# A gated DeltaNet layer on one core: another split of the PSUM banks and longer delays in a hand-set TensorE order

## The chip, the core and the metric

The kernel runs on one core of a Trainium2 chip. The core has five engines with instruction streams of their own: PE (TensorE, matrix products into PSUM), DVE (VectorE), ACT (ScalarE), POOL (GpSimd) and SP (SyncE, which here issues every DMA). The metric is the device time of one execution in microseconds (us), and the median over runs is compared.

## What is computed

One layer of a decoder trunk with 1024 tokens of 1024 features, 16 value heads and 8 query/key heads of 128 features, in chunks. Cut to what matters, for each head:

```python
hdn = rms_norm(x, norm_g) * (1 + scale) + shift
proj = hdn @ w_in                              # q, k, v, z, and the two gates
q, k, v = silu(causal_conv4(qkv))              # q and k normalised
a_mat = strict_lower((k * beta) @ k.T * decay) # a chunk's matrix
t_mat = inverse(a_mat + eye)
u, w = t_mat @ (v * beta), t_mat @ (k * beta * exp(gc))
for chunk in chunks:                           # the scan, state is 128 x 128
    v_new = u - w @ state
    o = q_dec @ state + qk @ v_new
    state = state * g_last + k_dec.T @ v_new
o = rms_norm(o) * silu(z)
x = rms_norm(x + gate * (o @ w_out), final_g)
```

## The kernel before

The 16 value heads form eight groups of two heads that share a pair of key and query heads. The work on a group is spread over *rounds*, gi = -1 to 7: while the scan of group gi runs, the inversion of group gi+1 and the projections for the groups gi+1 and gi+2 run between its steps. The rounds 2 to 5 are alike: each has 288 matmuls of projections.

A projection (`project`, L459) is 24 matmuls of 128x512 (eight slices of the features by three products of high and low parts) into one PSUM bank named `pj`, an accumulator. Behind it `Conv` works off the bank: ACT copies it (L442, xb) and multiplies it by a tap (L444, into vT for values and kq for keys and queries), DVE adds three taps (L446), ACT applies silu (L447). Weights come by SP (L139, wraw) and are split by ACT (L123, whi) and POOL (L124, wlo). A value tile vT is then turned by four PE transpositions (`turn`, L639) and scaled by DVE (L640, vtok).

The inversion of a group has two parts. `stage_a` makes the chunk matrices (L549), sends them through DRAM (L558) and loads them back as ua (L564); DVE then substitutes within 32x32 blocks in 31 steps (L575, L577), and the result goes through DRAM once more. `levels`, run once for each half of the chunks, joins the blocks: PE L603 and L605, then the negated copies pn by ACT (L609) and DVE (L610), PE L613 and L614, DVE copies L617 to L619, PE L622, ACT's negated copy pn2 (L625), PE L628.

`norms` loads the decays em, which ACT puts through exp (L499), and turns k and q (PE L508 and L515, ACT L510, L512, L518). `scan` has eight steps: PE L736 and L709, DVE r (L739), PE L755 into the bank `ts` with the inverse TT, then L762 and L767. `finish` turns an output with PE (L695) into a bank, ACT reads it (L697, oT), POOL multiplies it by z (L698), SP stores it (L699). In the last rounds `early` takes up the projection's bank with the first output products (L837).

[...] Before: two for `pj`, two for `tr` (all transpositions and the inversion's products), one each for `ks`, `oq`, `ts` and `pot`, the last for `finish` alone.

PE's order is written by hand: `drive` keeps a clock `now` of estimated ns. Each stream (scan, stage_a with levels, norms, residual_gate) yields a cost and a delay after each piece; when the clock has passed the delay, the stream has its next turn. In between `drive` takes single matmuls of the projections, the *fillers*, each 216 (MM). The delays are the constants D_*: D_N behind `norms`' q transpositions, D_L1 behind L603/L605, D_L2 behind L613/L614, D_L3 behind L622. A vT is turned when TURN filler matmuls have gone by since its projection's end. The other engines' orders are made by a scheduler from the program, and so shift when PE's does.

Of the kernel before, what the change touches and what calls it, by code (L numbers as in the profile page):

```python
# [9 lines left out]
F32 = mybir.dt.float32  # L10
# [7 lines left out]
P = 128  # L18
# [14 lines left out]
LAG, ZB, WGB = 3, 3, 1  # L33
EARLY, NLAST = 4, 3
NE = 15
TURN = 40
MM = 216

START, START1 = 11000, 65000
D_G, D_RG = 9500, 11000  # L40
D_N, D_A0, D_A = 3000, 1500, 1000
D_L0, D_L1, D_L2, D_L3 = 46000, 1600, 1800, 1600
D_R, D_V, D_S = 500, 1100, 700
D_F0, D_F = 8000, 2000

# [2 lines left out]
def gdn_layer(ctx: ExitStack, tc: tile.TileContext, x, c, ada_w, ada_b, norm_g, w_in, conv_w, a_log, dt_bias,  # L48
# [8 lines left out]
    nc = tc.nc  # L57
# [6 lines left out]
    TH = 512  # L64
# [65 lines left out]
    def load_w(c0, m, pool, hi_tag="whi", lo_tag="wlo", bufs=2):  # L130

        if c0 in ahead:
            return ahead.pop(c0)
        hi = pool.tile([P, KT, P], F32R, name=hi_tag, tag=hi_tag, bufs=bufs)
        lo = pool.tile([P, KT, P], F32R, name=lo_tag, tag=lo_tag, bufs=bufs)
        for k4 in range(0, KT, 4):
            ks = slice(k4, k4 + 4)
            raw = wpool.tile([P, 4, P], F32, name="wraw", tag="wraw", bufs=3)
            nc.sync.dma_start(out=raw[:, :, :m], in_=wv[:, ks, c0:c0 + m])  # L139
            split(raw[:, :, :m], hi[:, ks, :m], lo[:, ks, :m])  # L140
        return hi, lo
# [6 lines left out]


    pp = ctx.enter_context(tc.tile_pool(name="pp", bufs=1, space=PSUM))  # L150
    nbuf = {"pj": 2, "tr": 2}
    banks = ["pj", "pj", "ks", "oq", "ts", "pot"]

    def bank(tag, shape=(P, TH)):
        return pp.tile(list(shape), F32, name=tag, tag=tag, bufs=nbuf.get(tag, 1))
# [267 lines left out]
    cp = ctx.enter_context(tc.tile_pool(name="cp", bufs=2))  # L423
# [29 lines left out]
    def project(w, m, half):  # L453

        ps = bank("pj")
        hi, lo = w
        for k in range(KT):
            for n, (a, b) in enumerate(((hi, h_hi), (hi, h_lo), (lo, h_hi))):
                nc.tensor.matmul(ps[:m], lhsT=a[:, k, :m], rhs=b[half][k // 4][:, k % 4], start=(k == 0 and n == 0),  # L459
                                 stop=(k == KT - 1 and n == 2))  # L460
                yield MM
        return ps

    def trans():
        return bank("tr", (P, 4, P))
# [166 lines left out]
    def values(gi, G, more):  # L632

        G.vtok = []

        def turn(vT, h, hf):
            pv = trans()
            for j in range(4):
                nc.tensor.transpose(pv[:, j], vT[:, j * P:(j + 1) * P], ident)  # L639
            nc.vector.tensor_tensor(G.vtok[hf][:, :, h], pv, G.rinv[hf][:, :, None].to_broadcast([P, 4, P]),  # L640
                                    op=ALU.mult)

        def tiles():
            for h in range(2):
                ct = 16 + 2 * gi + h
                w = load_w(ct * P, P, wpool)
                cv = Conv(ct)
                for hf in range(NHALF):
                    if h == 0:
                        G.vtok.append(cp.tile([P, 4, 2, P], F32, name="vtok", tag="vtok", bufs=3))  # L650
                    ps = yield from project(w, P, hf)
                    vT = cp.tile([P, TH], F32, name="vT", tag="vT")
                    cv(ps, vT)
                    waiting.append((step[0] + TURN, vT, h, hf))

        waiting, step = [], [0]
        for cost in itertools.chain(tiles(), more or []):
            step[0] += cost / MM
            if waiting and step[0] >= waiting[0][0]:
                turn(*waiting.pop(0)[1:])  # L660
                yield 430
            yield cost
        for w in waiting:
            turn(*w[1:])
            yield 430
# [11 lines left out]
    def scan(gi, G):  # L677
# [12 lines left out]
                    nc.sync.dma_start(out=z, in_=z_dram[h0:h0 + 2, :, n * P:(n + 1) * P].rearrange("h e t -> e h t"))  # L690

        def finish(n, o):
            pot = bank("pot", (P, 2, P))
            for h in range(2):
                nc.tensor.transpose(pot[:, h], o[:, h], ident)  # L695
            oT = cp.tile([P, 2, P], F32, name="oT", tag="oT")
            nc.scalar.mul(oT, pot, normw_c)  # L697
            nc.gpsimd.tensor_tensor(oT, oT, zs.pop(n), op=ALU.mult)  # L698
            nc.sync.dma_start(out=o_dram[h0:h0 + 2, :, n * P:(n + 1) * P].rearrange("h e t -> e h t"), in_=oT)  # L699
# [25 lines left out]
        for n in range(NT):  # L725
# [4 lines left out]
            while len(late) > LAG:  # L730
                if can_finish():
                    finish(*late.pop(0))
                yield 0, 400
# [88 lines left out]
            ww.append((hl[0][:, s], hl[1][:, s]))  # L822
        return ww

    def load_g(kt, tg, hl, pool=cp, tag="vT", bufs=2):
        src = pool.tile([P, TH], F32, name="gsrc", tag=tag, bufs=bufs)
        nc.sync.dma_start(out=src, in_=o_dram[kt, :, tg * TH:(tg + 1) * TH])
        ghi, glo = hl
        nc.scalar.copy(ghi, src)
        nc.vector.tensor_tensor(glo, src, ghi.bitcast(F32), op=ALU.subtract)  # L830
        return ghi, glo
# [133 lines left out]

    gate_b, fg = rows32[:2]
    nc.sync.dma_start(out=fg, in_=final_g[None, :].to_broadcast([P, D]))
    banks = ["pj", "pj", "tr", "tr", "ks", "oq", "ts", "pot"]
    last = range(HV - NLAST, HV)
    wlast = None  # L970
    for tg in range(2):
# [64 lines left out]
```

## Time and profile before

| | |
|---|---|
| median of three runs | 1131.63 us (1130.09 to 1136.4) |
| the profiled execution | 1130.95 us |
| its span in the trace | 1129.2 us |
| mean granted TensorE clock | 0.979 |
| busy: PE, DVE, ACT, POOL | 1059.3, 745.1, 536.6, 450.0 us |

The span runs from the first to the last instruction. Busy time is what an engine spends in instructions other than waiting; a matmul's end is modelled. [...]

### The profile page before, as it was taken

The numbers are of one execution on the slowest core, as the hardware profiler recorded it, in microseconds if no ns is written. First come the engines' busy times: TensorE is split into PE (matmuls) and PEld (weight loads), VectorE is DVE, ScalarE is ACT, GpSimd is POOL, SyncE is SP. The second block draws the span as 40 slices with busy tenths as digits, with TensorE's granted clock in tenths as the row PEclk, the third lists the DMA queues.
The fourth block names the chain that finished last, engine by engine and source line by source line (L and its number), as shares of the span: only waits on it lengthen the run. The fifth ranks groups of instructions, "written<-read, shape, count | busy, mean of one in ns | idle before, by whom it ended". The sixth has DMA issues, their size and how long they took to land.

```text
span 1129.2 us, 18338 instructions
## 1 busy us (share of the span) xinstructions
PE 1059.3 (94%) x6295; PEld 857.6 (76%) x6295; DVE 745.1 (66%) x1914; ACT 536.6 (48%) x1416; POOL 450.0 (40%) x532
## 2 busy tenths in 40 slices
PE   8997999989999799999999999999899989999997
PEld 7875787767878678777877887788678768778785
DVE  5468775776579857865786677677766866513515
ACT  6567442453642455435543644364546424534523
POOL 3452223532444135323532452155216334954643
PEclk9998999999999999999999999999999989999999
DMA  9803333341145313421531143125313571446442
GB/s 287 234 19 133 75 82 85 101 126 43 39 135 164 83 50 100 125 56 30 145 102 45 42 146 84 39 54 163 74 29 103 149 219 63 140 135 185 152 121 75
DMA packets 188131, 119.48 MB, mean 106 GB/s; under 512 B 59733, under 2 KB 166534, under 8 KB 187014
## 3 DMA queue, kind: packets, MB, share of 16 engines
q1 hardware_dynamic: 187536, 118.20, 37.2%
q8 instruction: 50, 0.82, 0.3%
q14 instruction: 43, 0.35, 0.1%
q10 hardware_dynamic: 502, 0.10, 0.0%
HBM read 93.03 MB, written 25.24 MB: 105 GB/s over the span
## 4 chain that ended last, share of the span: by engine, by line
PE 41%; DVE 18%; ACT 6%; POOL 5%; DMA 4%; issue 4%; SPq 0%; POOLq 0%; DVEq 0%; ACTq 0%
PE pj L459 16%; PE pj L837 5%; DVE tb L577 4%; DVE tm L575 4%; DVE vT L446 3%; DVE em L497 3%; PE tr L549 2%; PE tr L837 2%; PE ts L755 2%; PE ks L736 1%; PE oq L709 1%; PE oq L762 1%; PE tr L622 1%; PE ks L767 1%; PE tr L628 1%
## 5 line engine op out<-in xcount | busy, mean ns | idle before, releaser
L124 POOL TENSOR_TENSOR wlo<-wraw,whi 128x512 fp32r<-128x512 f32 x92 | 126.1, 1379 | 147.3 <-ACT whi L123 107.7
L446 DVE SCALAR_TENSOR_TENSOR vT<-xb,taps,vT 128x512 f32<-128x512 f32 x96 | 84.6, 882 | 24.3 <-ACT vT L444 23.3
L446 DVE SCALAR_TENSOR_TENSOR kq<-xb,taps,kq 128x512 f32<-128x512 f32 x96 | 78.7, 828 | 12.9 <-ACT kq L444 11.0
L123 ACT CAST whi<-wraw 128x512 fp32r<-128x512 f32 x92 | 55.5, 618 | 64.9 <-PE pj L459 59.0
L577 DVE TENSOR_TENSOR tb<-tb,tm 128x126 f32<-128x126 f32 (+22 forms) x248 | 80.1, 323 | 4.8
L698 POOL TENSOR_TENSOR oT<-oT,z 128x256 f32<-128x256 f32 x64 | 50.6, 792 | 81.2 <-ACT oT L697 74.0
L575 DVE TENSOR_TENSOR tm<-tb,ua 128x126 f32<-128x126 f32 (+22 forms) x248 | 78.3, 316 | 6.2 <-DMA ua<-D 1.1
L459 PE MATMUL pj<-h1hia,whi 128*128 128x512 f32 x184 | 75.8, 412 | 6.6 <-ACT vT L444 6.6
L697 ACT ACTIVATE oT<-pot,cols 128x256 f32<-128x256 f32 x64 | 30.4, 474 | 108.1 <-PE pot L695 54.8
L459 PE MATMUL pj<-h0lob,whi 128*128 128x512 f32 x184 | 78.2, 425 | 0.0
L459 PE MATMUL pj<-h0hia,whi 128*128 128x512 f32 x184 | 76.8, 417 | 1.3 <-ACT kq L444 1.3
L459 PE MATMUL pj<-h1hib,whi 128*128 128x512 f32 x184 | 77.8, 423 | 0.0
L459 PE MATMUL pj<-h1lob,whi 128*128 128x512 f32 x184 | 77.7, 422 | 0.0
L459 PE MATMUL pj<-h1hia,wlo 128*128 128x512 f32 x184 | 77.5, 421 | 0.0
L459 PE MATMUL pj<-h0hib,wlo 128*128 128x512 f32 x184 | 77.1, 419 | 0.0
L459 PE MATMUL pj<-h1hib,wlo 128*128 128x512 f32 x184 | 76.6, 416 | 0.0
L459 PE MATMUL pj<-h0hia,wlo 128*128 128x512 f32 x184 | 75.8, 412 | 0.0
L459 PE MATMUL pj<-h1loa,whi 128*128 128x512 f32 x184 | 75.7, 411 | 0.0
L459 PE MATMUL pj<-h0loa,whi 128*128 128x512 f32 x184 | 75.6, 411 | 0.0
L459 PE MATMUL pj<-h0hib,whi 128*128 128x512 f32 x184 | 75.5, 410 | 0.0
L439 POOL MEMSET xb<- 128x3 f32 x32 | 3.4, 109 | 172.3 <-DVE kq L446 85.9
L719 POOL TENSOR_TENSOR sso<-sso,neg_half 128x2 f32<-128x2 f32 x64 | 44.6, 696 | 58.3 <-DVE sso L718 57.6
(445 smaller groups left out, 2933.1 us busy)
## 6 DMA issues: line engine op xcount, KB each, us to landing
wraw<-in_gdn_w_in SPq DMA_DIRECT2D x92, 256.0 KB, 2.9
woraw<-in_gdn_w_out SPq DMA_DIRECT2D x54, 256.0 KB, 3.2
wa<-in_ada_w SPq DMA_DIRECT2D x16, 512.0 KB, 6.9
em<-gc_dram SPq DMA_DIRECT2D x8, 1024.0 KB, 6.4
z_dram<-sz SPq DMA_DIRECT2D x32, 256.0 KB, 2.1
z<-z_dram SPq DMA_DIRECT2D x64, 128.0 KB, 2.4
o_dram<-oT SPq DMA_DIRECT2D x64, 128.0 KB, 1.9
gsrc<-o_dram SPq DMA_DIRECT2D x32, 256.0 KB, 2.9
```

What stands on the lines that cost most here:

```text
L123: nc.scalar.copy(hi, raw)
L124: nc.gpsimd.tensor_tensor(lo, raw, hi.bitcast(F32), op=ALU.subtract)
L446: nc.vector.scalar_tensor_tensor(dst, xb[:, j:j + TH], tp[:, j], dst, op0=ALU.mult, op1=ALU.add)
L459: nc.tensor.matmul(ps[:m], lhsT=a[:, k, :m], rhs=b[half][k // 4][:, k % 4], start=(k == 0 and n == 0), stop=(k == KT - 1 and n == 2))
L497: nc.vector.scalar_tensor_tensor(em[:, h, n], em[:, h, n], ngc[:, n, h0 + h:h0 + h + 1], mask, op0=ALU.add, op1=ALU.add)
L549: nc.tensor.matmul(pg2[:, 0:2], lhsT=kq[hf][:, 0, js], rhs=kq[hf][:, :, js], start=True, stop=True)
L575: nc.vector.tensor_tensor(tmv, tb[:, :mm, j:j + 1].to_broadcast([P, mm, ln]), ua[:, j:j + 1, j + 1:].to_broadcast([P, mm, ln]), op=ALU.mult)
L577: nc.vector.tensor_tensor(tb[:, :mm, j + 1:], tb[:, :mm, j + 1:], tmv, op=ALU.subtract)
L697: nc.scalar.mul(oT, pot, normw_c)
L698: nc.gpsimd.tensor_tensor(oT, oT, zs.pop(n), op=ALU.mult)
L719: nc.gpsimd.tensor_tensor(sso, sso, neg_half[:, :2], op=ALU.pow)
L837: nc.tensor.matmul(acc, lhsT=a[:, ts], rhs=b, start=(first and n == 0), stop=(last and n == 2))
```

## The change

The accumulator `pj` gets a third bank. It is the one that `pot` had; `finish` now turns its outputs in the bank `ts`, which the scan's L755 writes as well. vT gets a third buffer and is turned 56 fillers after its projection instead of 40. D_N grows from 3000 to 4000, D_L1 from 1600 to 2600, D_L2 from 1800 to 2200. load_g, which uses vT's buffers, has the same new count, the list of banks of the last product is put in another order, and a scratch area for DMAs is set to 1024 bytes.

```diff
-TURN = 40
+TURN = 56
...
-D_N, D_A0, D_A = 3000, 1500, 1000
-D_L0, D_L1, D_L2, D_L3 = 46000, 1600, 1800, 1600
+D_N, D_A0, D_A = 4000, 1500, 1000
+D_L0, D_L1, D_L2, D_L3 = 46000, 2600, 2200, 1600
...
-    nbuf = {"pj": 2, "tr": 2}
-    banks = ["pj", "pj", "ks", "oq", "ts", "pot"]
+    nbuf = {"pj": 3, "tr": 2}
+    banks = ["pj", "pj", "pj", "ks", "oq", "ts"]
...
-                    vT = cp.tile([P, TH], F32, name="vT", tag="vT")
+                    vT = cp.tile([P, TH], F32, name="vT", tag="vT", bufs=3)
...
-            pot = bank("pot", (P, 2, P))
+            pot = bank("ts", (P, 2, P))
...
-    def load_g(kt, tg, hl, pool=cp, tag="vT", bufs=2):
+    def load_g(kt, tg, hl, pool=cp, tag="vT", bufs=3):
...
-    banks = ["pj", "pj", "tr", "tr", "ks", "oq", "ts", "pot"]
+    banks = ["pj", "pj", "pj", "tr", "tr", "ks", "oq", "ts"]
...
-    nc = bacc.Bacc("TRN2", target_bir_lowering=False, num_devices=1)
+    nc = bacc.Bacc("TRN2", target_bir_lowering=False, num_devices=1, dynamic_dma_scratch_size=1024)
```

The order moves at three places that matter below, all alike in the rounds 2 to 5.

The first is the end of a round, the second half's last products of the inversion and the scan's first L755. PE before, with eight fillers (L459) between L622 and L628 and fourteen behind L628:

```order
L622 MATMUL tr<-TE,at 64x64 x8
L459 MATMUL pj<-h1hia,wlo 128x512
...
L628 MATMUL tr<-TT_757,pn_5153 64x64 x8
L459 MATMUL pj<-h1loa,whi 128x512
...
L755 MATMUL ts<-vtok,TT_756 128x128 x2
L508 MATMUL tr<-ident,kq 128x128 x4
```

and after:

```order
L622 MATMUL tr<-TE,at 64x64 x8
L459 MATMUL pj<-h1hib,wlo 128x512
L628 MATMUL tr<-TT_757,pn_5175 64x64 x8
L755 MATMUL ts<-vtok,TT_756 128x128 x2
L508 MATMUL tr<-ident,kq 128x128 x4
L515 MATMUL tr<-ident,kq 128x128 x4
```

One filler, the last of the round, is left between L622 and L628, and none behind. The others now stand earlier: 13 instead of 8 ahead of each L613, 11 instead of 7 to 9 ahead of each L622.

At the same place ACT, whose L625 makes the copy pn that L628 reads, before:

```order
L444 ACTIVATE kq<-pj,taps 128x512
L625 ACTIVATE pn_5153<-tr 64x512
L447 ACTIVATE kq<-kq 128x512
L123 CAST whi<-wraw 128x512
L442 COPY xb<-pj 128x512
L444 ACTIVATE kq<-pj,taps 128x512
L760 ACTIVATE vh<-ts,brk 128x128 x2
```

and after:

```order
L442 COPY xb<-pj 128x512
L444 ACTIVATE kq<-pj,taps 128x512
L625 ACTIVATE pn_5175<-tr 64x512
L123 CAST whi<-wraw 128x512
L447 ACTIVATE kq<-kq 128x512
L510 COPY ktok<-tr 128x512
L760 ACTIVATE vh<-ts,brk 128x128 x2
```

L625 has moved behind L442 and L444 of the round's last projection, and L510 stands ahead of L760.

The second place is DVE in the first half of the inversion, around L610, the copy that L614 on PE reads. Before:

```order
L640 TENSOR_TENSOR vtok<-tr,rinv 128x4x128
L441 COPY xb<-xb 128x3
L599 STREAM_TRANSPOSE TE<-TT_757 32x8x32
L446 SCALAR_TENSOR_TENSOR kq<-xb,taps,kq 128x512
L610 TENSOR_SCALAR pn<-tr 32x256
L446 SCALAR_TENSOR_TENSOR kq<-xb,taps,kq 128x512 x2
L617 COPY TT_756<-tr 32x8x32
```

and after:

```order
L441 COPY xb<-xb 128x3
L446 SCALAR_TENSOR_TENSOR kq<-xb,taps,kq 128x512 x2
L640 TENSOR_TENSOR vtok<-tr,rinv 128x4x128
L446 SCALAR_TENSOR_TENSOR kq<-xb,taps,kq 128x512
L610 TENSOR_SCALAR pn<-tr 32x256
L599 STREAM_TRANSPOSE TE<-TT_757 32x8x32
L617 COPY TT_756<-tr 32x8x32
```

L610 now follows all three L446 of a projection and an L640, and L599, which belongs to the other half, follows it.

The third place is SP's queue where ua is loaded (L564), in the middle of a round. Before:

```order
L690 DMA z<-z_dram 128x2x128
L674 DMA z_dram<-sz 128x512
L564 DMA ua<-D_6489 64x1024 x2
L699 DMA o_dram<-oT 128x2x128
L690 DMA z<-z_dram 128x2x128
L139 DMA wraw<-in_gdn_w_in 128x4x128 x2
```

and after:

```order
L558 DMA D_6504<-at 32x8x32 x4
L674 DMA z_dram<-sz 128x512
L139 DMA wraw<-in_gdn_w_in 128x4x128
L699 DMA o_dram<-oT 128x2x128
L564 DMA ua<-D_6504 64x1024 x2
L690 DMA z<-z_dram 128x2x128
L139 DMA wraw<-in_gdn_w_in 128x4x128
```

A load of weights and the store of an output (L699) now stand ahead of the load of ua.

Further, the second half's L508 of `norms` follows the second step's L755 and L762 instead of standing ahead of them; on DVE two L739 and one L711 of the scan stand ahead of the first L575 instead of behind it; DVE's passes on em (L497), which the exp L499 waits for, stand two steps of the substitution earlier.

## Rows read from the trace of the kernel before

**Rows 1.** The page, busy time of each engine, share of the span, instructions.
```profile
PE 1059.3 (94%) x6295; PEld 857.6 (76%) x6295; DVE 745.1 (66%) x1914; ACT 536.6 (48%) x1416; POOL 450.0 (40%) x532
```

**Rows 2.** PE waits for what: us in total, times, longest us.
```profile
PE pj L459 <- ACT vT L444: 6.6, 4, 1.7
...
PE tr L639 <- ACT vT L447: 6.0, 5, 2.6
...
PE tr L613 <- ACT pn L609: 3.9, 5, 0.8
PE tr L614 <- DVE pn L610: 3.8, 6, 0.7
...
PE tr L622 <- DVE TE L619: 2.2, 1, 2.2
```

**Rows 3.** Timeline of PE: start us, us, instruction, idle before and releaser.
```profile
634.13 0.65 PE L508 MATMUL tr<-ident,kq 128*128 128x128 f32 x4 [0.66 <-ACT tr L512]
```

**Rows 4.** Three rounds: us, PE, PEld, DVE, ACT, POOL busy, PE clock, DMA.
```profile
586.30:694.20 107.90, 103.26 (x650) 83.63 (x650) 75.69 (x204) 53.04 (x153) 39.69 (x51) 0.98 0.30 81
694.20:800.70 106.50, 101.78 (x650) 82.48 (x650) 75.64 (x204) 53.06 (x153) 39.70 (x51) 1.00 0.31 82
```

**Rows 5.** Chain that ended last, 548 to 608 us: start us, us, what.
```profile
551.49 0.49 SPq L564
...
604.34 0.44 DVE pn L610
605.51 1.98 PE pj L459 x6
```

**Rows 6.** Timeline of PE at the end of round 3.
```profile
621.14 1.14 PE L622 MATMUL tr<-TE,at 64*64 64x64 f32 x16
...
624.26 1.14 PE L628 MATMUL tr<-TT,pn 64*64 64x64 f32 x16
625.34 0.51 PE L459 MATMUL pj<-h1loa,whi 128*128 128x512 f32 x1
...
628.71 0.49 PE L755 MATMUL ts<-vtok,TT 128*128 128x128 f32 x3
```

**Rows 7.** Timeline of SP's queue after the load of ua.
```profile
554.33 0.37 SPq L699 DMA_DIRECT2D o_dram<-oT  x1
```

**Rows 8.** Timeline of DVE, scan inside the substitution.
```profile
557.47 0.34 DVE L739 SCALAR_TENSOR_TENSOR r<-ks,negc,vtok 128x128 f32<-128x128 f32 x1
...
558.25 0.41 DVE L711 TENSOR_TENSOR o<-o,oq 128x256 f32<-128x256 f32 x1
```

**Rows 9.** Timeline of DVE around L610.
```profile
601.64 0.69 DVE L640 TENSOR_TENSOR vtok<-tr,rinv 128x512 f32<-128x512 f32 x1
...
603.09 0.43 DVE L599 STREAM_TRANSPOSE TE<-TT 32x256 f32<-32x256 f32 x1
...
604.80 1.54 DVE L446 SCALAR_TENSOR_TENSOR kq<-xb,taps,kq 128x512 f32<-128x512 f32 x2
```

**Rows 10.** Timeline of ACT, exp of em and the projection behind it.
```profile
583.25 1.91 ACT L499 ACTIVATE em<-em 128x2048 f32<-128x2048 f32 x1
585.07 0.57 ACT L442 COPY xb<-pj 128x512 f32<-128x512 f32 x1
585.54 0.69 ACT L444 ACTIVATE vT<-pj,taps 128x512 f32<-128x512 f32 x1
```

**Rows 11.** Timelines of PE and ACT at the end of round -1.
```profile
181.73 0.97 PE L628 MATMUL tr<-TT,pn 64*64 64x64 f32 x13 [0.68 <-ACT pn L625]
...
181.09 0.59 ACT L625 ACTIVATE pn<-tr 64x512 f32<-64x512 f32 x1
```

**Rows 12.** A window behind L613 and L614, columns as in rows 4.
```profile
606.40:610.00 3.60, 3.60 (x22) 2.82 (x21) 1.94 (x4) 0.61 (x1) 0.11 (x1) 0.53 0.00 0
```

**Rows 13.** Timelines of ACT and PE, an output in round 3.
```profile
541.75 0.47 ACT L697 ACTIVATE oT<-pot,cols 128x256 f32<-128x256 f32 x1 [2.64 <-PE pot L695]
...
542.22 0.61 PE L755 MATMUL ts<-r,TT 128*128 128x128 f32 x4
```

## The prediction

> **What bounds the kernel now.** I read the totals first: TensorE (PE) is busy 1059.3 of 1129.2 us [rows 1], so the kernel can gain only where PE waits, and it must lose wherever the change makes PE wait. The list of PE's waits [rows 2] gives the places. Four of its rows come back once in each of the rounds 2 to 5, the rounds that are alike: the first matmul of a projection that needs an accumulator (6.6 us in four waits, some 1.65 each), the transposition of v (6.0 in five, one of them 2.6 in round 1, so about 0.85 in each of the four others), and L613 and L614, the second products of the inversion, which wait for the negated copies L609 on ACT and L610 on DVE (3.9 and 3.8). The transpositions of k wait 0.66 in such a round, at 634.13 [rows 3].
>
> Then I asked which of these waits the round's length depends on. The stretches from one round's accumulator wait to the next's are 107.9 and 106.5 us [rows 4]. The chain of work that ended last, followed back from the end of the first inversion half of round 3 [rows 5], passes from PE to SP's queue, to the load of ua at 551.49, through DVE's substitution, and over ACT and DVE to L610 at 604.34; only then is PE itself on it, from 605.51. So each such round has two parts in series. From 551 to 605 the chain is DMA, DVE and ACT, and a PE wait inside it (the accumulator, the transposition of v) is slack: take it away and PE waits at L614 instead. From 605 to the next load of ua PE is the chain, and every matmul and wait there counts in full, that at L508 too.
>
> **The change part by part.** A projection matmul costs 3.37 us / 14 = 0.24, from the 14 that lie between 625.34 and L755 at 628.71 [rows 6]; I use 0.235.
>
> *Third accumulator, third vT, TURN 56.* PE no longer stops for an accumulator, nor for the silu of v. Both waits are in the chain's first part, so in rounds 2 to 5 I cost their removal at nothing by itself. What hides it is the chain to L610; if that cover were gone it would be worth 1.65 + 0.85 a round.
>
> *D_L1 and D_L2 longer.* Rows of the order show 13 fillers instead of 8 ahead of L613 and 11 instead of 7 to 9 ahead of L622. Over the first half of the inversion and its approach 12 more matmuls are spent before L614, and 11 fewer are left between it and the round's end. The PE part becomes 11 x 0.235 = 2.6 us shorter per round, if L614 starts when it did.
>
> *When L614 starts.* Two things move L610 back. SP's order puts the load of ua behind L699, whose turn was 554.33 instead of 551.49 [rows 5, 7], so 2.8 us later; three DVE instructions of the scan that stood inside the substitution (L739 twice, 0.34 each, and L711, 0.41; together some 1.0 [rows 8]) now run before it, which leaves 1.8. And DVE's order puts two more L446 and an L640 ahead of L610, and takes L599 out: 1.54 + 0.69 - 0.43 = 1.8 [rows 9]. Upper bound 3.6. Lower bound 0.2: PE reaches L614 after 12 x 0.235 = 2.8 more work and 1.65 + 0.85 less waiting, if L610 is then ready. I take 1.4, in the lower half, because DVE's last passes on em stand two steps of the substitution earlier in the order, so the exp of em, 1.91 us that held ACT until 585.07 while the next projection's L442 stood behind it [rows 10], ends sooner after ua lands, and so do the conv passes that L610 now follows.
>
> *The round's end.* Here the fillers are missing. Before, eight matmuls covered the copy L625 between L622 (621.14) and L628 (624.26), and 14 more lay ahead of L755 [rows 6]. After, one matmul stands between L622 and L628, and none between L628 and L755. Where nothing covered L625 in the kernel before, in round -1, PE waited 0.68 us for it, and L625 itself took 0.59 [rows 11]. On ACT, L625 moreover now follows L442 and L444 of a projection whose last matmul is that single filler. So L628 starts after the filler's end (0.4), L442 0.47 by starts, L444 0.6 to 0.7 [rows 10], L625 0.59: 2.0 us of waiting. [...] I take 2.0; the bounds are 0.7 and 2.6 (with a whi cast of 0.6 also ahead).
>
> *D_N longer.* The second half's L508 now stands behind L755 and L762, which are 0.45 us of PE work each, so the 0.66 of [rows 3] is covered. It lies in the PE part: -0.66 a round. It could also be worth nothing if L515 inherits it.
>
> Rounds 2 to 5 together: (1.4 - 2.6 + 2.0 - 0.66) x 4 = **+0.6**.
>
> *The clock.* [...] After the change L614 waits about 0.2 to 3.6 us in one piece where it waited 1.5 in two, and the round's end gets a second such place, with small products, a wait and transpositions in a row. Rounds 2 to 5 now have two such windows that I read; I take two more, **+2.9**; bounds -2.9 (none is left) and +8.7 (six more).
>
> *The outputs in the inverse's bank.* finish() now writes its two transpositions where L755's product goes, so L755 waits until ACT's L697 has read them. Before, the read at 541.75 took 0.47, and L755 started at 542.22, just as it ended [rows 13]. In the 40 inner steps of this kind that stall is 0.08 us as I compare read and start, in two steps of round 7 about 0.8. That sums to 4.3; inside rounds 1 to 5 most of it lies ahead of L614's wait or in other slack, and I count round 7 and round 0: **+2.3** (bounds 0 and 4.3, and up to 16 if ACT is regularly late by 0.4).
>
> *Round 6.* In the after order L622 follows three matmuls (0.7) where L617 to L619 need 3 x 0.42, 1.25, and L628 follows none: 0.55 + 2.0 = **+2.5** (bounds 0 and 3).
>
> *Round 1 and round -1.* Round 1 has the longest v wait (2.6) and the one L622 wait (2.2) [rows 2]. Both get more cover; but as in the other rounds the inversion's chain stands behind the first. I take **-2.0**, between 0 and -4.8. In round -1 ten matmuls move from the inversion to the norms and the gram products, where they cover some 1.2 of waits, and L622 loses 7 matmuls of cover, 1.2: nothing.
>
> *The rest.* The bank names of the last product are only permuted, the smaller DMA scratch frees memory and removes no transfer, and load_g's third buffer lets two loads start earlier that PE did not wait for: 0; with that cover gone, the waits of early()'s products, which read such loads, would grow by what the loads come later.
>
> Sum: 0.6 + 2.9 + 2.3 + 2.5 - 2.0 = **+6.3 us** on the profiled execution's 1130.95, so 1137.2. The median of the three runs is 0.7 above that execution, so I leave it at **1137 us**.
>
> **The rivals.**
> *The listed waits come back (faster).* If ACT and DVE follow PE rather than lead it, so that L610 is ready whenever PE comes earlier, the waits fall out: 6.6 (accumulator) + 6.0 (v) + 4 x 0.66 (L508) + 7.7 (L613, L614) + 2.2 (L622) = 25.1, less the new ones 4 x 2.0, 2.5 and 4.3: -10.3, **1121 us**. For it speaks that the accumulator's wait repeats at the same place in four rounds. [...] Against it: the chain [rows 5] runs past that gap without touching it, and DVE's order in front of L610 got longer. It decides if L610 ends no later than 0.2 after its old place relative to the round. Chance 0.27.
> *Nothing moves.* L610 comes 0.6 later rather than 1.4, L628 waits 0.7, no clock windows are added: rounds (0.6 - 2.6 + 0.7 - 0.66) x 4 = -7.8, outputs +2.3, round 6 +1.3, round 1 0: -4.2, **1127** (to 1133, where part of the 2.0 stays). Chance 0.17.
> *The clock falls at both places of each round (slower).* Four rounds with two windows where now two rounds have one: six more, 8.7, with L614 late by 3 (4 x 1.6 more than I took, 6.4) : 6.3 - 2.9 + 8.7 + 6.4 = +18.5, **1149 us**. For it speaks that small products behind a wait now open such windows [rows 12]. Chance 0.16.
>
> **How the numbers follow.** My own case, 1132 to 1144, has 0.40, and its middle lies about on the bound between "no change" and "slower": 0.5%, 5.65 us, is about what a measurement of this kernel can tell from none. I give 0.18 of it to the same and 0.22 to slower. With the rivals: faster 0.27 + a corner of the unmoved case, 0.02; same 0.15 + 0.18 = 0.33; slower 0.22 + 0.16 = 0.38. The range for 8 in 10 leaves out the ends of the first and last rival: 1118 to 1148.
>
> **What would show it.** Right, if L459's accumulator wait and L639's are gone from the list, L614 has a wait of 1.5 us or more per round in their place, with L610 as its releaser, L628 shows about 2.0 us released by ACT's L625 at the end of rounds 2 to 5, and L508's wait is gone. Wrong, if the rounds 2 to 5 measure under 106 us each: then L610 followed PE, and the waits were the bound. Wrong the other way, if the granted clock falls in every round. The shared bank would show as waits at L755 released by L697, and at L695 released by the readers of ts.

## The result

The changed kernel takes 1171.35 us (median of four runs, 1167.44 to 1174.46) against 1130.86 of before: a ratio of 1.0335, 95% interval 1.03 to 1.037. The range ended at 1148; the direction of the sum was right, its size was not. The profiled execution is the fastest of the four, 1167.44, with a span of 1165.6 us, 36.4 more than before. The granted clock is the share of its full speed that the profile gives for PE's clock. The four runs have granted clocks of 0.961, 0.957, 0.952 and 0.957 in the order 1167, 1171, 1174, 1172 us: one program, longer by 7 us where the clock is lower.

PE's waits in the changed kernel, the same view as [rows 2] (us in total, times, longest):

```profile
PE tr L628 <- ACT pn L625: 8.9, 6, 1.9
PE tr L613 <- issue: 7.8, 4, 2.0
PE tr L622 <- DVE TE L619: 7.2, 5, 1.9
...
PE tr L614 <- DVE pn L610: 3.9, 5, 0.9
PE pj L837 <- POOL h0hib L811: 3.8, 1, 3.8
PE tr L793 <- DVE accg L231: 3.3, 1, 3.3
...
PE tr L515 <- DVE TT L629: 2.9, 3, 1.0
...
PE ts L755 <- ACT oT L697: 1.7, 2, 0.9
```

The accumulator's wait and that of the transposition of v for the silu are gone, as forecast. L628, L622 and L613 have grown, and L793 is new. Of these the sum had L628, the wait in front of the second products (at L614 rather than L613) and 0.55 at L622 in round 6; it had nothing for L622 elsewhere and nothing for L793.

The span cut at the first L755 of each scan, so that the second row is round 0 and the last one round 7 with the rest (columns as in [rows 4]):

```profile
0.00:187.00 187.00, 167.73 (x935) 136.76 (x935) 123.97 (x312) 100.58 (x209) 64.04 (x83) 0.95 0.50 138
187.00:306.60 119.60, 110.86 (x702) 88.16 (x700) 76.71 (x195) 46.08 (x115) 35.08 (x47) 0.94 0.26 69
306.60:424.80 118.20, 107.13 (x668) 85.53 (x667) 93.20 (x276) 55.39 (x156) 41.08 (x53) 0.99 0.38 103
424.80:534.70 109.90, 104.06 (x651) 83.60 (x650) 75.93 (x204) 53.68 (x153) 39.81 (x52) 0.98 0.31 81
534.70:647.40 112.70, 107.12 (x653) 86.74 (x651) 76.82 (x204) 53.57 (x152) 40.51 (x52) 0.94 0.30 79
647.40:756.40 109.00, 103.78 (x651) 84.60 (x650) 75.08 (x204) 53.56 (x152) 38.50 (x52) 0.98 0.30 79
756.40:868.60 112.20, 106.17 (x652) 86.00 (x650) 76.08 (x204) 53.56 (x152) 39.71 (x52) 0.95 0.30 78
868.60:974.10 105.50, 92.01 (x541) 73.50 (x539) 74.00 (x191) 45.46 (x142) 41.79 (x48) 0.94 0.50 147
974.10:1165.60 191.50, 180.05 (x860) 146.55 (x858) 78.54 (x129) 76.70 (x185) 106.39 (x98) 0.97 0.37 118
```

The same cuts in the kernel before give 183.6, 112.5, 115.2, 109.2, 108.2, 106.5, 106.5, 97.5 and 190.0 us, with granted clocks of 0.94, 0.97, 0.99, 0.98, 0.98, 1.00, 1.00, 0.96 and 0.99. So:

| stretch | predicted | measured |
|---|---|---|
| to the first L755 | 0 | +3.4 |
| round 0 | part of the bank's 2.3 | +7.1 |
| round 1 | -2.0 | +3.0 |
| rounds 2 to 5 | 0.6 + 2.9 (clock) | +13.4 |
| round 6 | +2.5 | +8.0 |
| round 7 and the end | part of the bank's 2.3 | +1.5 |
| sum | +6.3 | +36.4 |

In rounds 2 to 5 PE spends more time at half its clock: the trace has two stretches of 3.4 us before, and after it six, three of 3.4 and three of 6.8, in which every whole slice of 0.4 us has a granted clock of 0.50, together 6.8 us before and 30.7 after. At 0.50 half of that time is lost at most, 3.4 and 15.4, which bounds the clock's part at 12.0 of 13.4. Over the whole span length times one minus the granted clock is 23.7 (a clock of 0.979) and 45.5 (0.961), at most 21.8 of 36.4. Such a stretch is called a *window* below.

Two places of round 3 show what happens. The round's end, PE and then ACT (start, duration, idle before and releaser):

```profile
642.04 1.14 PE L622 MATMUL tr<-TE,at 64*64 64x64 f32 x16
643.11 0.49 PE L459 MATMUL pj<-h1hib,wlo 128*128 128x512 f32 x1
645.48 1.97 PE L628 MATMUL tr<-TT,pn 64*64 64x64 f32 x16 [1.88 <-ACT pn L625]
647.38 1.22 PE L755 MATMUL ts<-vtok,TT 128*128 128x128 f32 x4
```

```profile
643.64 0.58 ACT L442 COPY xb<-pj 128x512 f32<-128x512 f32 x1 [0.83 <-PE pj L459]
644.12 0.69 ACT L444 ACTIVATE kq<-pj,taps 128x512 f32<-128x512 f32 x1
644.84 0.59 ACT L625 ACTIVATE pn<-tr 64x512 f32<-64x512 f32 x1
```

L628 waits 1.88 us: the filler ends at 643.6, L442 and L444 of its projection come first on ACT, L625 only at 644.84. Then the granted clock of the stretch behind it:

```profile
644.80:651.60 6.80, 6.12 (x33) 5.72 (x33) 4.14 (x5) 3.80 (x13) 1.56 (x2) 0.50 0.29 78
```

It is at 0.50 for all of 6.8 us, and it reaches 4.2 us into round 4; [rows 6] had this place without a wait. The other place is the first join of the inversion, PE and then DVE:

```profile
622.32 0.22 PE L613 MATMUL tr<-TT,pn 32*32 32x32 f32 x2 [1.97 <-issue]
623.39 0.21 PE L614 MATMUL tr<-TT,pn 32*32 32x32 f32 x1 [0.85 <-DVE pn L610]
```

```profile
621.53 0.68 DVE L640 TENSOR_TENSOR vtok<-tr,rinv 128x512 f32<-128x512 f32 x1
622.13 0.74 DVE L446 SCALAR_TENSOR_TENSOR kq<-xb,taps,kq 128x512 f32<-128x512 f32 x1
622.90 0.43 DVE L610 TENSOR_SCALAR pn<-tr 32x256 f32<-32x256 f32 x1
```

L613 waits 1.97 us and the view names nobody, though ACT's L609 had run from 620.00 to 620.37. It starts 0.1 after L640 is done (621.53 + 0.68), the DVE reader of the bank of transpositions that L613 writes next; L614 waits on, 0.85, for L610. Both DVE instructions stand behind the L446 of the projection.

Where in a round the time goes is seen from the first L755 on, in round 4, which starts at 628.71 before and at 647.38 after. The load of ua on SP's queue and L614 before:

```profile
659.73 1.14 SPq L564 DMA_DIRECT2D ua<-D  x2
712.77 0.21 PE L614 MATMUL tr<-TT,pn 32*32 32x32 f32 x1 [0.69 <-DVE pn L610]
```

and after:

```profile
683.58 1.13 SPq L564 DMA_DIRECT2D ua<-D  x2
734.80 0.21 PE L614 MATMUL tr<-TT,pn 32*32 32x32 f32 x1 [0.86 <-DVE pn L610]
```

The load is issued 36.2 us into the round instead of 31.0, and L614 starts at 87.4 instead of 84.1. In the rounds 2 to 5 L614 comes 1.6, 4.3, 3.4 and 5.0 later, 14.2 together; what lies behind it is 0.8 shorter together. So the loss of these rounds lies ahead of L614.

### The profile page after: what moved, and what is told of

Its sections match the earlier page's. It is cut to its first block, busy times and chain, and to the rows that moved or that the text cites. A ratio compares the mean times of both kernels' runs of the same rounds, so it can differ in the third digit from the quotient of the medians.

```text
span 1165.6 us, 18318 instructions
## 1 busy us (share of the span) xinstructions
PE 1078.9 (93%) x6295; PEld 871.4 (75%) x6295; DVE 750.3 (64%) x1914; ACT 538.6 (46%) x1416; POOL 446.9 (38%) x532
## 3 DMA queue, kind: packets, MB, share of 16 engines
q1 hardware_dynamic: 187536, 118.20, 36.2%
## 4 chain that ended last, share of the span: by engine, by line
PE 42%; DVE 18%; POOL 5%; ACT 5%; issue 4%; DMA 4%; SPq 1%; POOLq 0%; DVEq 0%; ACTq 0%
PE pj L459 17%; PE pj L837 5%; DVE vT L446 4%; DVE tb L577 3%; DVE tm L575 3%; PE tr L837 2%; DVE kq L446 2%; DMA ua<-D 2%; DVE em L497 2%; PE tr L549 2%; PE ts L755 2%; PE tr L622 1%; PE ks L767 1%; PE ks L736 1%; PE oq L709 1%
## 5 line engine op out<-in xcount | busy, mean ns | idle before, releaser
L124 POOL TENSOR_TENSOR wlo<-wraw,whi 128x512 fp32r<-128x512 f32 x92 | 123.6, 1351 | 136.1 <-ACT whi L123 104.9
L446 DVE SCALAR_TENSOR_TENSOR kq<-xb,taps,kq 128x512 f32<-128x512 f32 x96 | 80.3, 844 | 31.3 <-ACT kq L444 30.0
L446 DVE SCALAR_TENSOR_TENSOR vT<-xb,taps,vT 128x512 f32<-128x512 f32 x96 | 83.9, 874 | 18.8 <-ACT vT L444 18.0
L575 DVE TENSOR_TENSOR tm<-tb,ua 128x126 f32<-128x126 f32 (+22 forms) x248 | 76.9, 310 | 14.2 <-DMA ua<-D 8.8
L697 ACT ACTIVATE oT<-ts,cols 128x256 f32<-128x256 f32 x64 | 30.3, 474 | 113.1 <-PE ts L695 59.4
L459 PE MATMUL pj<-h0hia,whi 128*128 128x512 f32 x184 | 80.2, 436 | 1.3 <-ACT kq L444 1.3
L459 PE MATMUL pj<-h0hia,wlo 128*128 128x512 f32 x184 | 79.8, 434 | 0.0
L459 PE MATMUL pj<-h1hib,wlo 128*128 128x512 f32 x184 | 78.9, 429 | 0.0
L123 ACT CAST whi<-wraw 128x512 fp32r<-128x512 f32 x92 | 55.4, 619 | 48.7 <-PE pj L459 41.1
L459 PE MATMUL pj<-h0hib,whi 128*128 128x512 f32 x184 | 77.8, 423 | 0.0
L459 PE MATMUL pj<-h0loa,whi 128*128 128x512 f32 x184 | 77.1, 419 | 0.0
L459 PE MATMUL pj<-h1lob,whi 128*128 128x512 f32 x184 | 76.5, 416 | 0.0
L459 PE MATMUL pj<-h1hia,whi 128*128 128x512 f32 x184 | 76.5, 416 | 0.0
L459 PE MATMUL pj<-h1loa,whi 128*128 128x512 f32 x184 | 76.3, 415 | 0.0
L459 PE MATMUL pj<-h1hia,wlo 128*128 128x512 f32 x184 | 76.0, 413 | 0.0
L459 PE MATMUL pj<-h1hib,whi 128*128 128x512 f32 x184 | 75.8, 412 | 0.0
L459 PE MATMUL pj<-h0lob,whi 128*128 128x512 f32 x184 | 75.2, 409 | 0.0
L459 PE MATMUL pj<-h0hib,wlo 128*128 128x512 f32 x184 | 74.5, 405 | 0.0
```

What stands on the lines that cost most here:

```text
L123: nc.scalar.copy(hi, raw)
L124: nc.gpsimd.tensor_tensor(lo, raw, hi.bitcast(F32), op=ALU.subtract)
L446: nc.vector.scalar_tensor_tensor(dst, xb[:, j:j + TH], tp[:, j], dst, op0=ALU.mult, op1=ALU.add)
L575: nc.vector.tensor_tensor(tmv, tb[:, :mm, j:j + 1].to_broadcast([P, mm, ln]), ua[:, j:j + 1, j + 1:].to_broadcast([P, mm, ln]), op=ALU.mult)
```

## The experiments

Times are medians. The kernel before ran in each group on the same chip (1130.6 to 1132.8), and the ratios are against it. "Rounds" are the cuts at the first L755, rounds 2 to 5.

### One part at a time

**banks_alone**: the third pj bank and the shared bank.

```diff
-    nbuf = {"pj": 2, "tr": 2}
+    nbuf = {"pj": 3, "tr": 2}
...
-            pot = bank("pot", (P, 2, P))
+            pot = bank("ts", (P, 2, P))
```

> Third pj bank, finish in the bank of L755, and the bank list of the last product; delays, TURN and vT as before, so PE's order is that of the kernel before. Theory A (the longer delays spend the fillers that covered the inversion's round end, and the clock falls there): the accumulator waits (6.6 us) go, most of it comes back at L614, the shared bank costs 2 to 5; 1128 to 1135 us, rounds 2 to 5 within 1.5 us of before, no additional half-clock windows. Theory B (the shared bank is the main cost): waits of L755 for L697 in every inner step, 2 us or more a round and so 12 to 20 us in all; 1142 to 1152.

1134.0 us, 1.0027 (0.9999 to 1.0056). The accumulator's 6.6 us are gone, and the waits at L639 have grown from 6.0 to 12.9. L755 waits 1.8 for L697. Rounds of 108.4, 107.1, 107.0, 107.2. The total is theory A's, but the wait came back at L639 and not at L614; the shared bank is cheap.

**inv_delays_alone**: `D_L1` 1600 to 2600, `D_L2` 1800 to 2200.

> Only D_L1 2600 and D_L2 2200. At the end of rounds 2 to 5 eight fillers are left ahead of L628 and none behind it; in round 6 and -1 L628 has none. Theory A: L628 keeps its cover in rounds 2 to 5, so there is a part of the loss only: rounds -1, 0 and 6 lose 3 to 8 us together, rounds 2 to 5 0 to 1.5 each with half-clock windows; 1134 to 1144. Theory B: 1129 to 1133, since neither bank is touched.

1146.3 us, 1.0136 (1.01 to 1.0173), above both theories. The rounds take 107.1, 107.0, 107.1, 106.9, no loss; round 0 loses 6.6, round 1 4.5, round 6 3.6, the start 2.9. Its largest wait:

```profile
PE tr L622 <- DVE TE L619: 9.5, 13, 1.8
```

L622 follows L614 with too little between, 13 times. L617 to L619, which it waits for, stand among other work on DVE: among the scan's and stage_a's in round 0 (L619 at 195.51), among three L446 of a projection in round 3 (L619 at 634.53).

**norm_delay_alone**: `D_N` 3000 to 4000.

> Only D_N 4000. The second L508 stands behind L755 and L762, 7 fillers instead of 14 are left behind L628, all 8 ahead of it stay. Theory A: L508's wait of 0.66 goes in rounds 2 to 5, nothing else is uncovered there, L628 is bare in rounds -1 and 6 only: 1128 to 1134. A theory in which the norms' new place itself (L515 waiting for a bank of transpositions) is the loss: L515 waits over 1 us in each round, 1136 to 1142.

1144.6 us, 1.0121 (1.0087 to 1.0156): both theories were wrong. The rounds are 107.4, 106.9, 107.1, 106.6, no loss and no wait at L515; round 1 loses 6.6, round 6 5.6, round 0 3.3.

```profile
PE ks L767 <- DVE vd L758: 8.2, 7, 1.5
PE tr L793 <- DVE accg L231: 7.1, 2, 3.8
```

L793, the residual gate's product in round 1, did not wait in the kernel before; now 7.1 us, for accg's sum on DVE (L231). The first time DVE makes it behind passes on em (355.4 to 359.1); the second time, 3.8 us, its L229 had waited 2.48 for the DMA that loads wag. Inside the rounds 2 to 5 the delay is not free either: the load of ua is issued 35.9 us into round 4 instead of 31.0, as in the changed kernel, and L614 comes 1.7 later on average, but the part behind L614 is shorter. Round 4 starts at 634.13 there, and:

```profile
670.00 1.13 SPq L564 DMA_DIRECT2D ua<-D  x2
```

**turn_alone**: `TURN` 40 to 56, third buffers of vT and gsrc, the small scratch.

> Only TURN 56 with the third vT and gsrc buffer and the small DMA scratch. Theory A: L639's waits (6.0 us) go, part of it comes back at L613 and L614; 1127 to 1132. A rival (the later transpositions push the DVE passes on v and with them L609, L610): L613 and L614 wait over 2.5 us together in each round, 1134 to 1142.

1129.3 us, 0.998 (0.9954 to 1.0005). L639's waits fall from 6.0 to 1.2, the accumulator's rise from 6.6 to 8.2, and L613 waits 5.2 for L610. The mirror of banks_alone.

### Parts together

**both_delays**: the edits of inv_delays_alone and norm_delay_alone.

> D_N 4000 and D_L1 2600, D_L2 2200 together, banks, vT and TURN as before. At the end of rounds 2 to 5 two fillers are left ahead of L628 and none behind it, as against eight with the inversion's delays alone. The delays one by one cost 14.7 and 13.1 us by medians, all of it in rounds -1, 0, 1 and 6; rounds 2 to 5 took about 107 us in both. Theory A (the loss in rounds 2 to 5 is the uncovered L628, which needs both delays at once): rounds 2 to 5 take 109 to 111 with L628 waiting 1.5 to 2 us for L625 and a half-clock window behind it; 1160 to 1170. Rival (the loss in rounds 2 to 5 comes with the banks or with TURN): rounds 2 to 5 stay at 107, the one-by-one losses add at most; 1148 to 1159.

1149.7 us, 1.0161 (1.0117 to 1.0204). Theory A fell: rounds of 107.4, 106.9, 108.0, 107.3 with two fillers ahead of L628. ACT, then PE at that place in round 3:

```profile
635.43 0.59 ACT L625 ACTIVATE pn<-tr 64x512 f32<-64x512 f32 x1 [2.76 <-PE tr L622]
636.05 0.59 ACT L442 COPY xb<-pj 128x512 f32<-128x512 f32 x1
```

```profile
634.20 1.14 PE L622 MATMUL tr<-TE,at 64*64 64x64 f32 x16
...
636.08 1.14 PE L628 MATMUL tr<-TT,pn 64*64 64x64 f32 x16
```

Here L625 stands ahead of L442 and L444, runs at once behind L622, and L628 does not wait. So two fillers and the first place in ACT's queue were enough here; where no filler is left at all, in the rounds -1 and 6, L628 still waits 0.68.

**turn_and_banks**: the change without its three delays.

> The whole change without the three longer delays: third pj bank, shared bank, third vT, TURN 56. One by one these moved the wait from the accumulator to the transposition of v (2.7 us) and from there to the accumulator (2.2). Theory A (L610 on DVE ends the round's first part, so neither edit nor both shorten it): accumulator and L639 waits both go and L613 and L614 wait 2 us or more in each round; rounds 2 to 5 at 105.5 to 107.5, 1127 to 1134. Rival (the two waits block each other's gain): both gone without a new one, rounds 2 to 5 at 104 to 105 us, 1118 to 1124.

1143.5 us, 1.011 (1.007 to 1.0151). One by one the two edits cost nothing or 3 us; together 12. In the waits the accumulator is gone, and:

```profile
PE tr L613 <- DVE pn L610: 13.2, 5, 2.9
...
PE tr L639 <- DVE vtok L640: 6.0, 5, 1.4
```

The waits moved to the join, the inversion's second products, as theory A said, 2.9 us in one piece in each of the four rounds. What it missed is the clock: 0.97 in each of them, which take 110.2, 109.1, 109.0, 109.1.

**after_short_inv** and **after_short_norm**: the changed kernel with `D_L1, D_L2 = 1600, 1800`, and with `D_N = 3000`.

> The changed kernel with D_L1 1600 and D_L2 1800 again; D_N stays 4000. Eight fillers stand ahead of L628 and eight behind it in rounds 2 to 5. Theory A: rounds 2 to 5 back at 106 to 108 us, no wait at L628 there; what D_N costs in rounds 0, 1 and 6 stays; 1138 to 1147. Rival (the shared bank makes the loss in rounds 2 to 5): 110 us a round, 1155 or more.

> The changed kernel with D_N 3000 again; D_L1 2600 and D_L2 2200 stay. Eight fillers stand ahead of L628 and none behind it in rounds 2 to 5. Theory A: the wait at L628 is 0 to 0.5 us, rounds 2 to 5 at 106.5 to 108.5; what the inversion's delays cost in rounds -1, 0, 1 and 6 stays; 1140 to 1150. Rival (bare place behind L628 and the shared bank make the loss): 110 us a round, 1158 or more.

1156.4 us, 1.0231 (1.0188 to 1.0275), with rounds of 111.1, 109.5, 110.2, 110.9; and 1152.1 us, 1.0184 (1.0147 to 1.022), with 108.6, 108.6, 108.6, 107.5. Theory A missed both, by 9 and 2 us, since turn_and_banks loses 12 by itself; after_short_inv came out as its rival forecast, though that does not show the rival's cause, the shared bank (L755 waits 0.6 for L697 in all). L628 does not wait in the rounds 2 to 5 of either; the join does.

**delays_mid_only** and **delays_edge_only**: the delays chosen by group.

```diff
-            yield 430, D_N
+            yield 430, 4000 if 3 <= gi <= 6 else 3000
```

and likewise at D_L1 and D_L2; the second kernel has `not 3 <= gi <= 6`.

> The changed kernel with the longer D_N, D_L1, D_L2 for the groups whose inversion runs in rounds 2 to 5 and the old ones in rounds -1, 0, 1 and 6. If the loss sits in the edge rounds (after minus before by stretches: -1, 0, 1, 6, 7 together 23.0 us, rounds 2 to 5 13.4), and the delays make it there, this kernel keeps what turn_and_banks loses in the edge rounds (about 6) and the 13 of rounds 2 to 5: 1148 to 1156. Rival (rounds 2 to 5 are where the delays cost): 1160 or more.

> The complement: the longer delays in rounds -1, 0, 1 and 6 only, the old ones in rounds 2 to 5, whose order is that of turn_and_banks. Edge rounds as in the changed kernel (23 us), rounds 2 to 5 as in turn_and_banks (109 each, 7 above before): 1160 to 1167. Rival as in delays_mid_only: 1150 or less.

1159.6 us, 1.0243 (1.0212 to 1.0274), and 1160.4 us, 1.0244 (1.0206 to 1.0283). The second came as expected, the first 4 us above. Against turn_and_banks the delays cost 16 and 17 us, and both halves at once 28: neither place is the whole. Two of the rounds of delays_mid_only:

```profile
530.10:643.10 113.00, 107.75 (x651) 87.76 (x650) 76.14 (x204) 53.64 (x152) 39.57 (x52) 0.94 0.29 78
643.10:755.70 112.60, 107.67 (x651) 87.71 (x650) 76.20 (x204) 53.63 (x152) 39.82 (x52) 0.94 0.29 78
```

Each of its last three full rounds has a clock of 0.94 and takes 112.5 to 113.0: the windows at both places, every round.

### Is it the clock?

Theory C says that a wait costs by the clock behind it rather than by its own length. The next kernels add matmuls of 128x512 that nobody reads, as one line, in rounds 2 to 5.

```diff
+        busy = lambda t, n: [t] + [nc.tensor.matmul(t.rearrange("p a b -> p (a b)"), lhsT=h_hi[0][0][:, 0, :P],
+                                   rhs=h_hi[0][0][:, 0], start=True, stop=True) for _ in range(n)]
...
-        px = v8(trans())
+        px = v8(busy(trans(), 10 if hf == 0 and 3 <= gi <= 6 else 0)[0])
```

**busy_at_join** is this edit in turn_and_banks; **busy_after** is it in the changed kernel with 8, and 8 at pc ahead of the second half's L628.

> turn_and_banks with ten matmuls of 128x512 more ahead of the first L613 of an inversion in rounds 2 to 5, products that nobody reads (weights and moving data from the resident h); 40 x 0.235 = 9.4 us of additional PE work. In turn_and_banks PE waits 2.8 us there for L610 and a window of 6.83 us at half clock follows in each of these rounds. Theory C (the gathered wait costs by the clock, not by itself): the useless work fits into the wait, the windows behind it go, rounds 2 to 5 fall from 109.1 to 106.5 to 107.5, and the kernel from 1143 to 1133 to 1137 although it does more. Rival (the waits and their place cost, the clock is a bystander): rounds 2 to 5 stay at 109 or grow by up to 2.4; 1143 to 1153.

> The changed kernel with eight unread 128x512 matmuls ahead of the first half's L613 and eight ahead of the second half's L628 in rounds 2 to 5, 64 x 0.235 = 15 us of additional PE work. Theory C: the waits at L613 and L628 (2.1 each) are filled, the half-clock windows in rounds 2 to 5 (30 us in all) mostly go; these rounds fall from 110.9 on average to 108 to 109.5, the kernel to 1157 to 1166. Rival: the rounds stay or grow; 1171 to 1185.

busy_at_join failed as a test: 1151.2 us, 1.0166 (1.0128 to 1.0205). The added products write px's bank, waited for it as L613 had, and ran behind the wait; rounds of 112.8, 110.5, 111.5, 113.6. busy_after: 1156.5 us, 1.0214 (1.0165 to 1.0264), 15 us less than the changed kernel with some 15 us more of PE work; rounds of 110.4, 108.9, 109.4, 108.8, the last three at a clock of 1.00. The spans of the two profiled executions differ by 9.0, of which 6.3 are in these rounds. Only the products at L628 ran inside a wait. Those at L613 write its bank and waited themselves, and here the view names the releaser that it lacked for L613, L640:

```profile
618.78 2.11 PE L588 MATMUL tr<-h0hia 128*128 128x512 f32 x8 [1.91 <-DVE vtok L640]
```

The windows behind L613 are gone here all the same. In l628_filled below, without these products, they stay; so products behind a wait of 1.9 were enough here, and behind the 2.9 of busy_at_join they were not.

**join_filled** is busy_at_join with the ten products in a free bank of pj, ahead of px's allocation: `busy(bank("pj", (P, 4, P)), 10)`.

> turn_and_banks with ten unread 128x512 matmuls ahead of the first L613 in rounds 2 to 5, now into a free pj bank, so that nothing holds them back (9.4 us of work). Theory C (the gathered wait costs by the clock): they run inside the 2.8 us that L613 waits for L610, the windows of 6.83 us at half clock behind them go, rounds 2 to 5 take 106.3 to 107.5 instead of 109.0 to 110.1; 1133 to 1138. Rival (the wait itself or its place costs): rounds at 109 or longer; 1142 to 1150.

1136.9 us, 1.0037 (1.0018 to 1.0055), where turn_and_banks has 1.011. In round 3 of turn_and_banks, then of join_filled, where the ten products run at 605.10, take 2.47 us, and leave L613 a wait of 0.62:

```profile
611.82 0.26 PE L613 MATMUL tr<-TT,pn 32*32 32x32 f32 x1 [2.93 <-DVE pn L610]
```

```profile
605.10 2.47 PE L588 MATMUL pj<-h0hia 128*128 128x512 f32 x10
608.18 0.21 PE L613 MATMUL tr<-TT,pn 32*32 32x32 f32 x1 [0.62 <-DVE pn L610]
```

Rounds 3 and 4 of turn_and_banks, then of join_filled:

```profile
527.30:636.40 109.10, 104.12 (x652) 83.63 (x651) 75.64 (x203) 52.96 (x153) 39.82 (x51) 0.97 0.30 80
636.40:745.40 109.00, 104.30 (x652) 83.81 (x651) 75.53 (x203) 52.95 (x153) 40.31 (x51) 0.97 0.30 81
```

```profile
523.80:631.60 107.80, 104.30 (x661) 83.95 (x660) 75.70 (x203) 52.99 (x152) 40.26 (x51) 1.00 0.31 81
631.60:739.30 107.70, 104.35 (x662) 83.98 (x661) 75.60 (x203) 53.01 (x153) 40.26 (x51) 1.00 0.30 81
```

40 products more, and each round is 1.2 to 1.4 us shorter, at a clock of 1.00 instead of 0.97. L613 starts at the same place in both, 84.5 and 84.4 us into round 3, so the gain lies behind it: 24.6 and 23.4 us to the round's end. That is theory C, in the rounds as in the total. But round 4 of the kernel before, also at 1.00, takes 106.5, with L613 at 83.1 and the same 23.4 behind it. So about half of what turn_and_banks loses against such a round is the clock; the other half is that L613 starts later.

**l628_filled**: the changed kernel with 8 products ahead of the second half's L628 alone.

> The changed kernel with eight unread matmuls ahead of the second half's L628 in rounds 2 to 5 only (7.5 us of work). Theory C: the 6.83 us windows at the round's end go, those of 3.41 behind L613 stay; rounds 2 to 5 take 108 to 110, 1156 to 1163. If the windows behind L613 are gone here too, the round's end sets them as well, and the rounds take 107 to 108: 1150 to 1156. Rival: no gain, 1168 or more.

1159.1 us, 1.0225 (1.0189 to 1.0261), within the expectation. L628's wait and the windows at the round's end are gone, those behind L613 stay:

```profile
532.50:641.80 109.30, 105.39 (x659) 85.30 (x658) 75.94 (x204) 53.53 (x152) 39.68 (x52) 0.98 0.30 80
641.80:751.30 109.50, 105.40 (x660) 85.29 (x658) 75.76 (x204) 53.49 (x152) 39.76 (x52) 0.98 0.30 80
```

**pj_wait_filled**: turn_alone with 8 such products in the bank pot ahead of the projection that waits for its accumulator.

> turn_alone with eight unread 128x512 matmuls in the idle bank pot ahead of the projection whose first matmul waits 2.2 us for an accumulator in rounds 2 to 5. Theory C: the wait is filled, the windows of 3.41 us at half clock behind it (480, 586 and 692 us) go, these rounds take 105 to 105.5 instead of 106.3 to 107.6; 1122 to 1127, faster than before by 0.4 to 0.8%. Rival: no change of the rounds, 1128 to 1133.

1136.4 us, 1.0036 (1.0013 to 1.0059), slower than turn_alone. The accumulator's wait shrinks from 2.05 to 0.2 and the windows behind it are gone, but L613 waits 2.6 for L610 instead, with a window behind that in three of the four rounds; rounds of 110.2, 108.7, 108.8, 107.7. Both sides were wrong: the rounds are longer than the rival's. ACT's order shifted as well (a cast of weights, L123 at 598.59, now stands ahead of L442), so how much of it the products make is open.

### The bank of transpositions

**after_tr3** and **turn_tr3**: the changed kernel and turn_alone with `nbuf = {"pj": 2, "tr": 3}`, outputs in ts.

> The changed kernel with three tr banks and two pj banks. If L613 waits for the tr bank that L640 reads: its wait of 2.0 us and those of L603 and L515 (0.8 and 1.0) shrink to under 1 in rounds 2 to 5. Since L610 comes only 0.6 after L640, L614 would then wait for L610 instead, and the rounds keep 109 to 112; accumulator waits of about 2 return: 1160 to 1172. Rival (the bank is the cause of the lateness, L610 follows): rounds at 107 to 108, 1150 to 1158.

> turn_alone with the third tr bank, outputs in the bank ts. Theory (DVE's order ends the round's first part, whichever bank is added): rounds 2 to 5 as in turn_alone plus 0.5 to 1 for the shared bank, 106.8 to 108; 1129 to 1135. Rival (a third bank for the transpositions removes what a third accumulator only moved): rounds at 105 to 106, 1120 to 1127.

after_tr3: 1152.7 us, 1.0192 (1.0155 to 1.0228). L613 does not wait in the rounds any more; but PE reaches it later than in the changed kernel (614.9, L640 having ended at 612.8), so this run does not show that the bank was the reason. In its place:

```profile
PE pj L459 <- ACT vT L444: 10.6, 4, 3.0
PE tr L628 <- ACT pn L625: 8.9, 6, 1.9
```

The four accumulator waits are 10.6 us now, and the rounds take 109.6, 110.6, 109.5, 109.6, as the first expectation had them, while the total is the rival's; L610 was no longer waited for either. turn_tr3: 1135.9 us, 1.0044 (1.0016 to 1.0071), 1 us above what the theory allowed and far from the rival; its rounds of 107.3, 110.4, 108.9, 108.9 are longer than either said. No version here is measurably faster than the kernel before; turn_alone comes nearest.

## Why the prediction was wrong

The steps that failed are the price of the clock in the rounds 2 to 5 and the terms for the rounds at both ends, which were nearly nothing.

**The first part of the round** (*Third accumulator, third vT, TURN 56*): right that the removed waits come back. banks_alone moves them to L639, turn_alone to the accumulator, turn_and_banks to L613, after_tr3 back to the accumulator. The releaser was only half named: in the changed kernel L613 waits for L640's bank (named in busy_after), and L610 adds 0.85.

**The round's end**: right in place, releaser and size. L628 waits 1.88 where 2.0 was forecast. That L625 would not start before L442 and L444, which stand ahead of it, was the author's assumption; in this trace it held: L625 starts at 644.84, when L444 (644.12, 0.69 long) is done. With L625 ahead of both, in both_delays, the wait is nil.

***When L614 starts***: 1.4 a round was taken, 5.6 in the four, and 14.2 was measured. The windows behind L628 have 6.8, 4.2 and 6.8 us of their length in the rounds 3, 4 and 5, so at most 9.0 of the 14.2 is the clock's; the other 5.2 are close to the forecast. The way to it was not: the load of ua came 4.9 later with the longer D_N alone, where the sum had 2.8 from SP's order, and more of that was made up again. In l628_filled, without these windows, L614 comes 1.9 later on average.

***D_N longer*** inside the rounds 2 to 5, -0.66 each: L508's wait is gone, but L515 waits 0.9 and 1.0 for L629 in the rounds 3 and 5, which the text had allowed for.

**The clock**: the step that failed in rounds 2 to 5. It took two more windows of the length that [rows 12] shows, +2.9, at 1.45 each, an estimate from what the two stretches of [rows 4] differ by (107.9 less 106.5). No run shows that as the cost of one window; what the runs showed in its place is the 1.3 us a round of join_filled below. The trace has four more windows, and three of its six are twice as long: 12.0 at most. Without the clock's part 1.4 is left of the 13.4, where the sum had 0.6. The third rival, windows at both places of each round, is what delays_mid_only shows in full and the changed kernel in the rounds 2 and 3. The prediction's own sign of being wrong this way, a clock that falls in every round, came in three of the four (0.94, 0.98 and 0.95 where before had 0.98, 1.00 and 1.00). This sum itself put waits of 2 us at two places of each round; but a count of windows could not be read off, since the waits of 0.78 and 0.69 ahead of the window of [rows 12] stand in the rounds 4 and 5 of before as well, at a clock of 1.00. join_filled shows that the clock costs 1.3 us a round in turn_and_banks (1.00 against 0.97 with the same wait filled), and l628_filled and busy_after that the changed kernel's rounds get shorter by 4.4 and 6.3 together with more PE work in them.

***Round 1 and round -1*** and ***Round 6***, at 0.5 us together, with nothing for D_N outside the rounds 2 to 5: the larger failure, some 21 us with round 0. The sum took the rounds that are alike as the kernel and the others by one or two waits. Measured alone, D_N costs 13 us and the inversion's delays 14.7, all of it outside rounds 2 to 5, with waits at L793, L767 and L622, where other streams (the scan's first steps, the residual gate) stand in the places that the fillers left. That L622 lost its fillers in round -1 stood in the text, at 1.2 us; what L793 and round 0 would do was not looked at. At most 9.8 of the 23.0 us outside rounds 2 to 5 is the clock's.

**The outputs in the inverse's bank**: +2.3 was forecast (40 times 0.08 and twice 0.8 make 4.8, not 4.3, which moves only a bound and the first rival). L755 waits 1.7 for L697 in the changed kernel and 1.8 in banks_alone, all in round 7, so the size holds; the total of banks_alone, 2.4 above its reference, is not clear of noise.

What stays open: why the parts do not add up (2.4 for the banks, -2.3 for TURN, 13.1 and 14.7 for the delays make 28, the change has 40). The first two together cost 12, of which filling the join's wait gives back 6.5; the remaining 28 are the delays upon them. Of delays_mid_only's 16 us above turn_and_banks some 13.5 lie in the four rounds. What makes a wait bring a window is open too: those of 1.95 and 0.86 at the join brought one in the rounds 2, 3 and 5 of the changed kernel and none in round 4, in the one execution that was traced.

## What to carry to other kernels

In these runs a wait removed upstream of a join was a wait moved (12.9 us at L639 in banks_alone, 13.2 at L613 in turn_and_banks); it cost most where several short ones had become one of 2 to 3 us in front of small products (12 us in turn_and_banks, with 2.9 in one piece), so price the granted clock with the wait, at every place where the sum itself puts one. In an order that is set by hand with estimated times, a longer delay takes cover from another stream: before pricing the steady rounds, walk through the first and last ones and list what loses its cover there. A delay also moves what its own stream does next, here the load that starts the next chain. And look at which instruction stands first in the copying engine's queue, not only at how many matmuls are ahead of the waiting one.

## What the runs showed of the hardware

More PE work made the kernel shorter: 64 unread products of 128x512 took 15 us off the changed kernel by the medians (9.0 between the profiled executions). Where the wait of 2.9 us was filled (join_filled), the windows were gone in all four rounds, each at a clock of 1.00; where the products ran behind that wait (busy_at_join), the clock stayed at 0.94 to 0.98, though behind a wait of 1.9 (busy_after, rounds 3 to 5) it was 1.00. The same wait does not always bring a window: 2.56 us at L639 in banks_alone did in three of the four rounds, the clock of the fourth is 1.00.
